# Output projections of a hybrid decoder block: residual with tokens on partitions, two projections by seven products, and weight parts made by accumulating DMAs

## The chip, the cores and the metric

The kernel runs on one core of a Trainium2 chip. The metric is the time of one execution on the device in microseconds; it is compared by the median of several runs. Engines are named as in the profile: PE is TensorE (matmuls; PEld its weight loads), DVE is VectorE, ACT ScalarE, POOL GpSimd, SP SyncE.

## What is computed

One decoder block on 512 tokens of width 1024, in float32, then a final norm:

```python
h = h + hybrid_mixer(rmsnorm(h), ...)            # 1024 -> ... -> [y_ssd | y_pool] (2048) @ w_out (2048 x 1024)
h = h + memory_cross_attention(rmsnorm(h), rmsnorm(mem), w_q, w_kv, w_o)   # 4 heads into 256 memory tokens
h = h + swiglu(rmsnorm(h), w_gate_up, w_down)    # width 2816
return rmsnorm(h, final_norm)
```

In the mixer, the first half of the concatenation, `y_ssd`, is a gated state-space result under an RMS norm of its own; the second, `y_pool`, comes from causal pooling. So the mixer's output is `rmsnorm(y) @ w_out[:1024] + y_pool @ w_out[1024:]`. Three matrices of 1024 x 1024 are the subject here: the pool half of `w_out` (stage **op**), its state-space half (**os**), and the attention's `w_o` (**wo**).

## The kernel before

**Precision.** Every float32 product is three TensorE matmuls of fp32r parts: high by high, high by low, low by high (`mm3`, L116). A weight block of 128 x 1024 (a *unit*) is loaded by SP into a `raw` buffer; ACT casts it to `whi` (L203) and DVE takes the difference as `wlo` (L205). There are 6 `raw`, 4 `whi` and 5 `wlo` buffers. Activations are split alike (`splits`: names end in h and l).

**Order.** `SPEC` is a table of slots; a slot is a line of items such as `os:3` or `k:0`. While the matmuls of a slot run, `advance` prepares the units of the next one, and the finishing steps (`post`) of the slot's items are woven between. Matmuls of one engine run in the order of the program.

**Strassen.** The FFN (stages g and d) and the attention's values (v) take seven products of half matrices in place of eight (`product`). Their weight blocks are four quarters of the matrix, numbered as forms 1 to 7; forms 3, 5, 6 and 7 are sums of quarters. The sums are made by an accumulating DMA that POOL issues (L172 loads a second quarter onto a `raw` buffer; L211 adds form 5 to form 1 and makes form 6 in a `wq` buffer) or by DVE (L190, L194: form 3). The activations' forms are made by `forms` (L1176). The products gather in the PSUM banks A (forms 1, 6, 7, 4), B (5, 3) and C (2), and DVE adds each bank to its two quarters of the result (`INTO`).

**The stages around the change** (with the time at which their matmuls begin in the profile):

- `op` (206.9): eight units, each 24 matmuls of 128 x 512. The result has features on partitions; `xT`, the input transposed, is added to it (L798).
- `os` (253.9): the same with `y`, which has been scaled and split before (`t_ygh`, `t_ygl`). The norm of `y` is a sum over partitions by two matmuls with ones (`ry`, L299) whose 128 x 512 result multiplies each unit's output (L329); L817 adds it to the residual. That is split for the attention (`t_hg`), and squares are added up for the next norm (`hacc`).
- `k` (297.7), `q` (321.0): keys and queries; the sums for the next norm (`r2`, two ones-matmuls) and four transposes (`r2t`) stand among them. Then the scores of four heads, their softmax, transposes of the probabilities (`pT`), and the products with the values (`o`, 12 matmuls for each half of a head).
- `wo` (410.0): eight units of 24; DVE adds each to the residual (L1048), ACT scales it for the FFN (L1054), and `forms` makes the FFN's forms. Between the last units the residual is turned by 32 transposes (`hT`, L1222) so that tokens are on partitions, as the FFN's drains want it, and its squares are summed by row.
- The FFN begins at 455.4 with product 1 of gate block 0 (`gA`).

Of the kernel before, what the change touches and what calls it, by code (L numbers as in the profile page):

```python
# [61 lines left out]
def hybrid_block(ctx: ExitStack, tc: tile.TileContext, a: dict, out: bass.AP,  # L62
# [119 lines left out]

    def split_unit(key):
        n = units[key][1]
        raw = ready[key]
# [21 lines left out]
        if key[0] == "s" and f == 2 and CHUNKS[c][:2] != ("g", 5):  # L207
            if (c, 5) not in sw:
                load_strassen(("s", c, 5))
            sw[c, 6] = sw.pop((c, 1))  # L210
            nc.gpsimd.dma_start(sw[c, 6][:, :n], sw[c, 5][:, :n], accum_op=ALU.add)  # L211
# [575 lines left out]
    def i_op(m):  # L787
        it = Item(keys=[("op", m)])

        def prep():  # L790
            it.x = T("x2")
            nc.sync.dma_start(it.x, a["xT"][m * P:(m + 1) * P, :])

        def mm():
            proj(hold(it, "op"), ready[("op", m)], [st["pg", k] for k in range(8)])

        def post():
            nc.vector.tensor_tensor(out=it.x, in0=it.x, in1=it.ps, op=ALU.add)  # L798
            st["hp", m] = it.x

        it.prep, it.mm, it.post = prep, mm, post
        return it

    rmsy = Rms("ry", "yacc")
    rms2 = Rms("r2", "hacc")
# [20 lines left out]


# [114 lines left out]
    def i_r2t():  # L942
        it = Item()

        def mm():
            pt = hold(it, "r2t")
            for c in range(NC):
# [611 lines left out]
```

## Time and profile before

| | us |
|---|---|
| median of 3 runs | 793.7 (793.55 to 793.85) |
| the profiled execution | 794.94 |
| its span on the core | 793.1 |
| mean granted TensorE clock in it | 0.997 |
| matmuls of `op` | 206.9 to 253.3 |
| matmuls of `os` | 253.9 to 297.5 |
| matmuls of `wo` | 410.0 to 454.8 |

A row of the groups reads: line, engine, operation, output and inputs by the program's names, shapes, count; then total busy time and mean duration in ns; then the idle time of the engine ahead of them and what ended it. A matmul's duration is longer than the step from one to the next, since they overlap. The time of a DMA is from its issue to its landing.

### The profile page before, as it was taken

How to read it: one execution, taken by the hardware profiler on the slowest of the kernel's cores; microseconds unless marked ns; L12 is line 12 of the kernel's file. 1: busy time of each engine (PE TensorE's matmuls, PEld its weight loads, DVE VectorE, ACT ScalarE, POOL GpSimd, SP SyncE). 2: the span in 40 equal slices, each digit the busy share in tenths (PEclk: the TensorE clock that was granted, in tenths of full speed). 3: DMA queues.
4: the chain of work that ended last, by engine and by line, in shares of the span. 5: the costliest groups of instructions: out<-in, count | busy, mean ns of one | idle time of the engine just before them, and what ended most of it. 6: DMA issues, size and time to landing. Idle time of an engine off the chain costs nothing.

```text
span 793.1 us, 10458 instructions
## 1 busy us (share of the span) xinstructions
PE 782.3 (99%) x3789; PEld 655.9 (83%) x3789; DVE 635.4 (80%) x944; ACT 499.6 (63%) x803; POOL 49.8 (6%) x66
## 2 busy tenths in 40 slices
PE   9999999999999999999999999999999999999996
PEld 7878888888888888888888888888888888888984
DVE  7999879999895798875766667788857798867897
ACT  8667699657953547555655695665445575455855
POOL 0000000000000000000000011011101011101000
PEclk9999999999999999999999999999999999999998
DMA  9235326134474234765455268787869798879702
GB/s 336 86 110 177 114 86 179 54 105 127 158 262 161 93 107 149 171 188 165 132 126 145 68 142 232 173 242 160 250 143 297 162 248 181 239 157 264 177 14 106
DMA packets 41283, 128.60 MB, mean 162 GB/s; under 512 B 4865, under 2 KB 7297, under 8 KB 41233
## 3 DMA queue, kind: packets, MB, share of 16 engines
q1 hardware_dynamic: 32880, 99.04, 36.9%
q0 software_dynamic: 8064, 28.58, 20.2%
q8 instruction: 29, 0.48, 0.2%
q10 hardware_dynamic: 288, 0.33, 0.1%
q14 instruction: 22, 0.17, 0.1%
HBM read 116.63 MB, written 2.13 MB: 150 GB/s over the span
## 4 chain that ended last, share of the span: by engine, by line
PE 84%; DVE 9%; DMA 3%; ACT 2%; issue 2%; SPq 0%; DVEq 0%
PE gA L1104 14%; PE gB L1104 8%; PE dA L1104 4%; PE gC L1104 3%; PE dB L1104 2%; DVE wlo L205 2%; PE vAB L1104 2%; PE k L889 2%; DVE t_hT L1263 2%; PE op L117 2%; PE wo L119 2%; PE op L118 2%; PE wo L117 2%; PE q L118 2%; PE q L117 2%; PE os L118 2%
## 5 line engine op out<-in xcount | busy, mean ns | idle before, releaser
L203 ACT CAST whi<-raw 128x1024 fp32r<-128x1024 f32 (+1 forms) x125 | 129.0, 1040 | 90.6 <-PE wo L118 11.8
L205 DVE TENSOR_TENSOR wlo<-raw,whi 128x1024 fp32r<-128x1024 f32 (+1 forms) x125 | 150.0, 1208 | 28.2 <-ACT whi L203 27.3
L203 ACT CAST whi<-wq 128x1024 fp32r<-128x1024 f32 (+1 forms) x76 | 77.4, 1028 | 74.5 <-PE dA L1104 17.8
L205 DVE TENSOR_TENSOR wlo<-wq,whi 128x1024 fp32r<-128x1024 f32 (+1 forms) x76 | 90.3, 1194 | 38.8 <-ACT whi L203 38.6
L172 POOL DMA_DIRECT2D raw<-w_s x38 | 32.7, 865 | 646.4 <-DMA raw<-w_s 521.6
L1104 PE MATMUL gA<-whi,t_xh 128*128 128x512 f32 (+1 forms) x192 | 71.7, 373 | 0.0
L1104 PE MATMUL gA<-wlo,t_xh 128*128 128x512 f32 (+1 forms) x192 | 71.4, 372 | 0.0
L1104 PE MATMUL gA<-whi,t_xl 128*128 128x512 f32 (+1 forms) x192 | 71.3, 371 | 0.0
L1104 PEld LDWEIGHTS gA<-whi,t_xh 128*128 128x128 f32 x192 | 36.2, 188 | 6.3
L1104 PEld LDWEIGHTS gA<-wlo,t_xh 128*128 128x128 f32 x192 | 36.2, 188 | 6.3
L1104 PEld LDWEIGHTS gA<-whi,t_xl 128*128 128x128 f32 x192 | 36.2, 188 | 6.1
L1120 ACT ACTIVATE t_gu<-t_gu,s 128x512 f32<-128x512 f32 (+1 forms) x24 | 16.4, 687 | 34.9 <-DVE t_gu L1116 34.9
L194 DVE TENSOR_TENSOR wq<-wq,wq 128x1024 f32<-128x1024 f32 (+1 forms) x19 | 22.5, 1194 | 16.7 <-DMA wq<-raw 16.7
L1104 PE MATMUL dA<-whi,t_xh 128*128 128x512 f32 (+1 forms) x91 | 34.7, 385 | 0.5 <-DVE t_hT L1263 0.3
L1104 PE MATMUL dA<-whi,t_xl 128*128 128x512 f32 (+1 forms) x91 | 34.8, 382 | 0.0
L1104 PE MATMUL dA<-wlo,t_xh 128*128 128x512 f32 (+1 forms) x91 | 34.6, 382 | 0.0
L1104 PE MATMUL gB<-whi,t_xq 128*128 128x512 f32 (+1 forms) x96 | 27.6, 371 | 0.0
L117 PE MATMUL z<-t_uh,whi 128*128 128x512 f32 x64 | 25.2, 394 | 0.6 <-ACT t_uh L233 0.6
L1182 ACT CAST t_xh<-t_x 128x512 fp32r<-128x512 f32 x30 | 18.6, 621 | 10.6 <-DVE t_x L1201 6.4
L117 PE MATMUL wo<-t_oh,whi 128*128 128x512 f32 x64 | 25.2, 394 | 0.0
L117 PE MATMUL v<-t_uh,whi 128*128 128x512 f32 x64 | 25.1, 392 | 0.0
L117 PE MATMUL q<-t_hgh,whi 128*128 128x512 f32 x64 | 25.1, 392 | 0.0
(406 smaller groups left out, 2224.6 us busy)
## 6 DMA issues: line engine op xcount, KB each, us to landing
raw<-w_u SPq DMA_DIRECT2D x68, 512.0 KB, 3.4
raw<-w_s SPq DMA_DIRECT2D x54, 512.0 KB, 4.5
wq<-w_s SPq DMA_DIRECT2D x36, 512.0 KB, 5.6
raw<-w_s POOLq DMA_DIRECT2D x36, 512.0 KB, 7.1
wq<-raw POOLq DMA_DIRECT2D x17, 512.0 KB, 8.2
t_x<-xT SPq DMA_DIRECT2D x16, 256.0 KB, 5.3
t_abc<-d_acs SPq DMA_DIRECT2D x16, 256.0 KB, 5.1
out<-t_hT SPq DMA_DIRECT2D x7, 256.0 KB, 2.1
```

Of the source, the lines that this page charges most:

```text
L117: nc.tensor.matmul(ps, whi, xhi, start=start, stop=False)
L118: nc.tensor.matmul(ps, whi, xlo, start=False, stop=False)
L119: nc.tensor.matmul(ps, wlo, xhi, start=False, stop=stop)
L172: nc.gpsimd.dma_start(sw[c, f][:, :n], quad("11" if f == 7 else "22"), accum_op=ALU.add)
L194: add = nc.vector.tensor_tensor(out=sw[c, 3][:, :n], in0=sw[c, 3][:, :n], in1=sw[c, 6][:, :n], op=ALU.add)
L203: nc.scalar.copy(hi[:, :n], raw[:, :n])
L205: nc.vector.tensor_tensor(out=lo[:, :n], in0=raw[:, :n], in1=hi.bitcast(F32)[:, :n], op=ALU.subtract)
L889: nc.tensor.matmul(it.ps[d], wh[:, ws], both, start=k == 0, stop=False, skip_group_check=True)
L1104: nc.tensor.matmul(it.ps[tt][:, o:e], p[:, ts_], w[:, ws], start=first, stop=(c, i, n) == pairs[-1] and p is xh and w is wl, skip_group_ch ...
L1120: st["silu"] = nc.scalar.activation(g, g, AF.Silu, scale=st["r3",][:, c:c + 1])
L1182: nc.scalar.copy(h if w is None else h[:, w], src)
L1263: d = nc.vector.tensor_tensor(out=h[:, half], in0=h[:, half], in1=it.ps[tt][:, half], op=ALU.add if sign > 0 else ALU.subtract)
```

## The change

The residual is kept with tokens on partitions from the start: eight tiles `h[c, r]` (128 tokens, half the features), loaded from `x` instead of `xT`.

- **op** stays plain but has tokens on its output's partitions: a unit covers two of eight feature blocks and one half of the output, and goes into four PSUM banks (`op`), which are drained into `h` after four units.
- **os becomes y, wo becomes o**, each by seven products (24 matmuls each, in the B and A and C banks; B is the double bank `pd`). The scaled `y` and the attention's outputs get their forms from a new function, `natural_forms`. The norm of `y` is four matmuls of one column and a short chain on 128 x 4 numbers (`rsqrt`); it is multiplied in by the drain. Form 1 and some others are cut into two items (`y:1.0`, `o:7.1`), one for each unit.
- **The features come back to partitions** for the attention by 32 new transposes (`hgT`), and for the FFN by the 32 of `hT`, now in the other direction. The sums of squares come from ACT on `h` (`sq`); the matmuls of `r2` and the transposes `r2t` are gone.
- **Low parts by DMA.** For 14 units (the last four of `op`, forms 7 and 4 of y and of o, form 5 of the first gate block) ACT casts the weight to `hi` as before, writes its negative, rounded alike, into `lo`, and POOL adds the raw weight to `lo` by an accumulating DMA. `early` starts them up to three units ahead.
- **Sums by DMA.** Form 3 of y, o and the first gate block is made by a third accumulating DMA (`wq<-wq`, L218) in place of the DVE addition.

```diff
+DMA_LOW = [('op', 4)]
+DMA_LOW_FORMS = {'y0': (4, 7), 'o0': (4, 7), 'g0': (5,)}
+DMA_SUM = ('y0', 'o0', 'g0')
...
-    "P:7", "op:0 g:5 op:1 op:2 g:6", "op:6 g:4 op:3 g:7", "op:5 op:4 ys", "op:7 yr", "os:0 ml", "os:1", "os:2",
-    "os:3 mm", "os:4", "os:5", "os:6", "os:7", "k:0", "k:1 r2", "k:2 vf:0", "k:3 rt vf:1", "q:0 vf:2 vf:3", "q:1 V:1", "q:2 V:2",
-    "q:3 S:0 V:5", "q:4 V:6",  "q:5 S:1 T:0 V:3", "q:6 S:2 T:1", "q:7 V:7 T:2", "V:4 S:3 O:0", "O:1", "T:3 O:2", "O:3", "o:0", "o:1",
...
+    "P:7", "op:0 g:5 op:1 op:2 g:6", "op:3 g:4 op:4 g:7 yf:0", "op:5 op:6 yf:1", "op:7 yf:2", "yr yf:3 ml", "y:1.0", "y:2.0", "y:5.0",
+    "y:1.1 y:2.1", "y:5.1 mm", "y:6", "y:3", "y:7 hg:0 hg:1", "y:4 hg:2 hg:3", "k:0", "k:1 hg:4 hg:5", "k:2 hg:6 hg:7 vf:0 sq:2.0",
+    "k:3 vf:1 sq:2.1", "q:0 vf:2 vf:3", "q:1 V:1", "q:2 V:2",
+    "q:3 S:0 V:5", "q:4 V:6",  "q:5 S:1 T:0 V:3", "q:6 S:2 T:1", "q:7 V:7 T:2", "V:4 S:3 O:0", "O:1", "o:1.0 T:3 O:2",
+    "o:5.0 O:3", "o:2.0", "o:1.1 o:2.1", "o:5.1", "o:6", "o:3", "o:7.0", "H:0 H:1 o:7.1", "H:2 H:3 o:4.0", "o:4.1",
...
+    def early(key):
...
+        hi = whi_p.tile([P, 1024], F32R, tag="hi", name=nm("whi"))
+        lo = wlo_p.tile([P, 1024], F32R, tag="lo", name=nm("wlo"))
+        nc.scalar.copy(hi[:, :n], raw[:, :n])
+        nc.scalar.activation(lo[:, :n], raw[:, :n], AF.Copy, scale=-1.0)
+        nc.gpsimd.dma_start(lo.bitcast(F32)[:, :n], raw[:, :n], accum_op=ALU.add)
...
+        if f in (2, 5) and CHUNKS[c][0] + str(CHUNKS[c][1]) in DMA_SUM and (c, 6) in sw and (f == 5 or (c, "5") in sw):
+            sw[c, 3] = sw.pop((c, 2))
+            nc.gpsimd.dma_start(sw[c, 3][:, :n], sw[c, 6][:, :n], accum_op=ALU.add)
...
-            t = mul("ot", it.ps, st["ry",])
-            h = st["hp", m]
-            nc.vector.tensor_tensor(out=h, in0=h, in1=t, op=ALU.add)
...
+                nc.vector.scalar_tensor_tensor(out=h, in0=it.ps[tt], scalar=st["ry",][sign][:, c:c + 1], in1=h,
+                                               op0=ALU.mult, op1=ALU.add)
...
+        H1 = cast(E, a_)
+        HO = cast(O)
+        M = T("x57")
+        nc.vector.tensor_tensor(out=M[:, a_], in0=E[:, a_], in1=E[:, b_], op=ALU.subtract)
+        nc.vector.tensor_tensor(out=M[:, b_], in0=O[:, b_], in1=E[:, b_], op=ALU.subtract)
+        yield
+        rest(H1[:, b_], E[:, a_], H1[:, a_])
+        LO = T("xl", F32R)
+        rest(LO, O, HO)
...
+        H2 = cast(M)
+        N = T("x64")
+        nc.vector.scalar_tensor_tensor(out=N[:, a_], in0=M[:, a_], scalar=-1.0, in1=O[:, b_],
...
+        nc.vector.scalar_tensor_tensor(out=N[:, b_], in0=N[:, a_], scalar=-1.0, in1=O[:, a_],
...
+        H3 = cast(N)
+        L2 = T("xl", F32R)
+        rest(L2, M, H2)
...
+        L3 = T("xl", F32R)
+        rest(L3, N, H3)
...
+            for key in plan[spos:spos + 3]:
+                early(key)
```

What this moves, at three places. In the program's order PE has 3756 matmuls instead of 3776, DVE 991 instructions instead of 946, ACT 814 instead of 774.

**PE, the end of os.** Before, the last unit of `os` is followed at once by the first key matmuls:

```order
L117 MATMUL os_2935<-t_ygh_2290,whi_2877 128x512
L118 MATMUL os_2935<-t_ygl_2293,whi_2877 128x512
L119 MATMUL os_2935<-t_ygh_2290,wlo_2878 128x512
L889 MATMUL k_2987<-t_mn_2769,whi_2918 128x512
L890 MATMUL k_2987<-t_mn_2769,wlo_2919 128x256
```

Now, at the change from product 7 of y to product 4 (`whi_605`, `wlo_606` and `whi_608`, `wlo_609` are the two units of form 4; both low parts come by DMA):

```order
L1213 MATMUL yA_563_2668<-wlo_595_2819,t_xh_534_2560 128x512
L948 MATMUL hgT_612_2945<-ident_88,t_h_451_2177 128x128
L948 MATMUL hgT_612_2945<-ident_88,t_h_452_2179 128x128
L948 MATMUL hgT_612_2945<-ident_88,t_h_453_2182 128x128
L948 MATMUL hgT_612_2945<-ident_88,t_h_454_2184 128x128
L948 MATMUL hgT_613_2950<-ident_88,t_h_451_2177 128x128
L948 MATMUL hgT_613_2950<-ident_88,t_h_452_2179 128x128
L948 MATMUL hgT_613_2950<-ident_88,t_h_453_2182 128x128
L948 MATMUL hgT_613_2950<-ident_88,t_h_454_2184 128x128
L1213 MATMUL yA_562_2667<-whi_605_2878,t_xh_490_2295 128x512
L1213 MATMUL yA_562_2667<-whi_605_2878,t_xl_496_2310 128x512
L1213 MATMUL yA_562_2667<-wlo_606_2879,t_xh_490_2295 128x512
```

The transposes of the residual's first half stand inside the y stage, and `wlo_609` is read nine matmuls into product 4.

**PE, the head of wo.** Before, the last head's attention product is wholly ahead of `wo`, which starts from the first head's parts:

```order
L119 MATMUL o_4070<-t_Ph_4043,t_Vl_3975 128x512
L117 MATMUL o_4070<-t_Ph_4045,t_Vh_3893 128x512
L118 MATMUL o_4070<-t_Pl_4056,t_Vh_3893 128x512
L119 MATMUL o_4070<-t_Ph_4045,t_Vl_3901 128x512
L117 MATMUL wo_4089<-t_oh_3971,whi_4051 128x512
L118 MATMUL wo_4089<-t_ol_3989,whi_4051 128x512
```

Now the first o product begins after head 1's attention product (`o_887`), ahead of the last head's probability transposes (`pT`), and the two are woven (`t_xh`, `t_xl` are forms of the attention's output):

```order
L125 MATMUL o_887_4116<-t_Ph_828_3895,t_Vl_746_3510 128x512
L123 MATMUL o_887_4116<-t_Ph_829_3897,t_Vh_797_3777 128x512
L124 MATMUL o_887_4116<-t_Pl_840_3920,t_Vh_797_3777 128x512
L125 MATMUL o_887_4116<-t_Ph_829_3897,t_Vl_808_3800 128x512
L1213 MATMUL oA_901_4152<-whi_868_4066,t_xh_876_4083 128x512
L1213 MATMUL oA_902_4153<-whi_868_4066,t_xh_876_4083 128x512
L1123 MATMUL pT_903_4166<-ident_88,t_p_865_4059 128x128 x2
L1123 MATMUL pT_903_4166<-ident_88,t_p_875_4080 128x128 x2
```

Four more matmuls of `oA`, four transposes `pT_904` and the first three of `oB` follow, then head 2's attention product. Two heads' attention products (24 matmuls) have moved behind the first matmuls of the projection.

**POOL, from wo into the FFN.** Before, its queue held second loads onto `raw` and two sums for the first gate block:

```order
L172 DMA raw_926_4307<-w_s 128x1024
L172 DMA raw_952_4419<-w_s 128x1024
L172 DMA raw_992_4574<-w_s 128x1024
L172 DMA raw_997_4596<-w_s 128x1024
L211 DMA wq_904_4206<-raw_926_4307 128x1024
L172 DMA raw_1024_4743<-w_s 128x1024
L211 DMA wq_935_4353<-raw_952_4419 128x1024
```

Now, from o's form 7 (`wlo_956`, `wlo_961`) over form 4 (`wlo_966`, `wlo_969`) to form 5 of the first gate block (`wlo_990`, `wlo_1026`):

```order
L205 DMA wlo_956_4371<-raw_937_4279 128x1024
L205 DMA wlo_961_4383<-raw_945_4307 128x1024
L205 DMA wlo_966_4420<-raw_948_4341 128x1024
L178 DMA raw_1040_4721<-w_s 128x1024
L178 DMA raw_1046_4748<-w_s 128x1024
L205 DMA wlo_969_4453<-raw_951_4349 128x1024
L205 DMA wlo_990_4551<-raw_964_4416 128x1024
L215 DMA wq_954_4368<-raw_964_4416 128x1024
L218 DMA wq_959_4380<-wq_954_4368 128x1024
L205 DMA wlo_1026_4678<-raw_975_4499 128x1024
```

`wlo_969` stands behind two second loads, the later of which goes into a buffer that `wlo_961` reads; `wlo_1026` stands behind two sums, and the second sum waits for the first. POOL's queue has 32 more DMAs in all.

More of the change, by code (lines that the diff above doesn't have):

```diff
@@ L206, in split_unit @@
         ready[key] = (hi, lo)
[L207 to L211, printed above, removed]
+        if key[0] == "s":
+            sums(key)
         yield
@@ L794, in mm @@
         def mm():
[L795 to L805 removed]
+            if k == 0:
+                st["op"] = [PS("op") for _ in range(NC)]
+            it.ps = st["op"]
+            wh, wl = ready[("op", j)]
@@ new lines, in mm @@
+            for c in range(NC):
+                cs = slice(c * P, (c + 1) * P)
+                for n in range(2):
+                    ws = slice(512 * n, 512 * n + 512)
+                    xh, xl = st["pg", 2 * k + n]
+                    mm3(it.ps[c], xh[:, cs], xl[:, cs], wh[:, ws], wl[:, ws], k == 0 and n == 0, k == 3 and n == 1)
+        def post():
+            for c in range(NC):
+                h = st["h", c, r]
+                nc.vector.tensor_tensor(out=h, in0=h, in1=it.ps[c], op=ALU.add)
+                yield
@@ new lines, in post, with i_y @@
+            st["ry",] = {1: p, -1: n}
+        it.mm, it.post = mm, post
+        return it
+    def i_y(f, part=None):
+        it, ends, _ = product("y", 0, f, part)
+        def post():
+            yield from need("ry")
+            r, k, sign = INTO[f]
+            for tt in range(2):
+                c = 2 * k + tt
+                h = st["h", c, r]
+                nc.vector.scalar_tensor_tensor(out=h, in0=it.ps[tt], scalar=st["ry",][sign][:, c:c + 1], in1=h,
+                                               op0=ALU.mult, op1=ALU.add)
+                yield
+        it.post = post if ends else None
+        return it
@@ L824, in i_os, with i_hg, mm, post @@
+    def i_hg(m):
+        it = Item()
+        def mm():
+            pt = hold(it, "hgT")
+            for c in range(NC):
+                nc.tensor.transpose(pt[:, c * P:(c + 1) * P], st["h", c, m // 4][:, (m % 4) * P:(m % 4 + 1) * P], ident)
+        def post():
+            yield from splits([("hg", m)], [("hg", 512)], [it.ps], col(V_XAT + m))
         it.mm, it.post = mm, post
@@ L940, in i_q @@
         return it
[L942 to L947, printed above, removed]
-                nc.tensor.transpose(pt[:, c * P:(c + 1) * P], st["r2",][:, c * P:(c + 1) * P], ident)
-        def post():
-            s = SM("r2s", [P, NC])
-            nc.vector.tensor_scalar(out=s, in0=it.ps.rearrange("p (c l) -> p c l", l=P)[:, :, 0],
-                                    scalar1=1.0 / 16.0, scalar2=None, op0=ALU.mult)
-            st["r2s",] = s
-        it.mm, it.post = mm, post
-        return it
     def i_score(h):
@@ L1497, in _pack @@
     wo = g["w_out_mix"]
-    u += [mtile(wo[1024:], m) for m in range(8)]
-    u += [mtile(wo[:1024], m) for m in range(8)]
+    wp = wo[1024:].reshape(4, 2, P, 2, 512)
+    u += [wp[k, :, :, r].transpose(1, 0, 2).reshape(P, 1024) for r in range(2) for k in range(4)]
     wkv = g["w_kv"]
@@ L1502, in _pack @@
     u += [mtile(g["w_q"], m) for m in range(8)]
-    u += [mtile(g["w_o"], m) for m in range(8)]
     w_u = np.stack([f(t) for t in u])
```

201 lines of the change are left out of this document (135 added, 66 removed), and 3 rows, old and new, of the table SPEC.

## The prediction

> **What bounds the kernel now.** I read the page's busy times first, then TensorE's waits, then a table of stretches.
>
> ```profile
> PE 782.3 (99%) x3789; PEld 655.9 (83%) x3789; DVE 635.4 (80%) x944; ACT 499.6 (63%) x803; POOL 49.8 (6%) x66
> ...
> PE 84%; DVE 9%; DMA 3%; ACT 2%; issue 2%; SPq 0%; DVEq 0%
> ...
> PE warm L384 <- DVE ones L100: 1.2, 1, 1.2
> PE z L117 <- ACT t_uh L233: 0.6, 1, 0.6
> PE yo L119 <- DVE t_prl L241: 0.4, 1, 0.4
> PE dA L1104 <- DVE t_hT L1263: 0.3, 1, 0.3
> PE gB L1104 <- DVE wlo L205: 0.2, 1, 0.2
> ```
>
> TensorE is busy in 99% of the span and 84% of the chain that ended last is its own. All its waits on other engines come to 2.7 us (the five rows added). So a matmul taken away comes off the time, as long as the engines that feed it still keep up; and there is nearly no wait left to remove. How near the feeders are to their limit stands in the stretches (columns: PE, PEld, DVE, ACT, POOL busy, then clock, DMA share, GB/s):
>
> ```profile
> 170.00:206.90 36.90, 36.49 (x190) 30.98 (x189) 34.71 (x59) 28.43 (x59) 0.00 (x0) 1.00 0.42 131
> 206.90:253.90 47.00, 47.00 (x220) 39.36 (x220) 35.11 (x51) 27.52 (x46) 0.00 (x0) 1.00 0.60 212
> 253.90:297.70 43.80, 43.80 (x195) 36.28 (x195) 36.05 (x58) 22.77 (x36) 0.00 (x0) 1.00 0.30 97
> 388.70:410.00 21.30, 21.24 (x113) 18.07 (x112) 17.70 (x30) 15.48 (x28) 1.70 (x2) 1.00 0.65 173
> 410.00:455.40 45.40, 45.40 (x210) 37.54 (x209) 26.08 (x42) 23.69 (x44) 2.55 (x3) 1.00 0.37 93
> ```
>
> The second row is `op`, the third `os`, the last `wo`. In all three TensorE never stops and its granted clock is 1.00. VectorE has 12 us to spare beside `op`, 8 beside `os`, 19 beside `wo`; 2.2 in the stretch ahead of `op`.
>
> **What the change takes from TensorE.**
>
> ```profile
> L117 PE MATMUL os<-t_ygh,whi 128*128 128x512 f32 x64 | 24.9, 389 | 0.0
> L117 PE MATMUL wo<-t_oh,whi 128*128 128x512 f32 x64 | 25.2, 394 | 0.0
> ...
> 474.05 5.44 PE gA L1104 x24
> ...
> L299 PE MATMUL ry<-t_ryh,ones_r x1: 389/389/389, 253.5 to 253.5; 128*128 128x512 f32 x1
> L948 PE MATMUL r2t<-ident,t_r2t x4: 270/272/273, 320.6 to 320.9; 128*128 128x128 f32 x4
> 458.38 0.87 PE hT L1222 x8
> ```
>
> `os` and `wo` are three lines of 64 matmuls each, 192 apiece. Seven of eight products are left, 168 apiece, of the same size: 48 fewer. A matmul lasts 389 ns, but they overlap: 24 back to back take 5.44 us in the chain, so 0.2267 us is what one costs. That is 48 x 0.2267 = **10.9 us**. The norms' sums go too: two 512-wide matmuls for `ry`, two alike for `r2`, 4 x 0.2267 = 0.9; and four transposes `r2t`. Eight transposes take 0.87, so 0.109 each: 0.4. Added are 32 transposes `hgT` (3.5 us) and four matmuls of one column for `ry`. The profile has no such matmul; it costs between nothing and a 512-wide one, so 0 to 0.9 for the four; I take the rate of a transpose, which also loads 128 columns, 0.4. The turn `hT` keeps its 32. `op` changes its layout but keeps 8 x 24 matmuls. Sum: 10.9 + 0.9 + 0.4 - 3.5 - 0.4 = **8.3 us** less TensorE work.
>
> **What the feeders must do now.** The rows that price it:
>
> ```profile
> L205 DVE TENSOR_TENSOR wlo<-raw,whi 128x1024 fp32r<-128x1024 f32 x122 | 148.0, 1221 | 28.2 <-ACT whi L203 27.3
> L1186 DVE TENSOR_TENSOR t_xl<-t_x,t_xh 128x512 fp32r<-128x512 f32 x30 | 19.9, 686 | 0.3
> L243 DVE SCALAR_TENSOR_TENSOR t_ygl<-t_y,vec,t_ygh 128x512 fp32r<-128x512 f32 x8 | 6.0, 747 | 0.1
> L241 DVE TENSOR_TENSOR t_ol<-o,t_oh 128x512 fp32r<-128x512 f32 x8 | 5.4, 689 | 2.5 <-ACT t_oh L233 2.4
> L1191 DVE TENSOR_TENSOR t_x<-t_fa,t_fb 128x256 f32<-128x256 f32 x15 | 6.3, 421 | 1.2 <-ACT t_fa L1169 0.9
> L203 ACT CAST whi<-raw 128x1024 fp32r<-128x1024 f32 x122 | 127.5, 1050 | 90.6 <-PE wo L118 11.8 <-PE gA L1104 10.8 <-PE op L118 10.5
> ```
>
> *Beside `op`*: a set of natural forms is five 256-wide and three 512-wide VectorE operations, 5 x 0.421 + 3 x 0.686 = 4.2 us; `yf` brings four sets, 16.6 us. Four low parts leave for the DMA (4 x 1.22 = 4.9). 35.1 + 16.6 - 4.9 = 46.8 of 47.0 us. That is full by mean durations; back to back a 512-wide operation costs some 0.60 (below, 1.29 for two), about a tenth less, and work may reach ahead into the y stage. The eight `ygl` (6.0 us) fall away too, but most of them stand ahead of this stretch, so I credit none. I count no wait here and keep it as a rival. *Beside y*: 14 low parts instead of 8, four of them by DMA, so 2.4 us more, while 14 drains at about 0.7 take the place of 16 operations on `os`; it stays inside the 8 us spare, which is the cover; without it, it would cost its own 2.4. ScalarE gains 14 casts against 8 and four copies for the DMA, 10 x 1.05, beside 21 us spare. *Beside o*: 16.6 for its forms instead of 5.5 for the eight `t_ol` at 0.69, six more drains (4.1), 2.4 of low parts: 17.6 more against 19 spare, and part of it stands already in the stretch ahead. These cost nothing.
>
> *The third y product.* The order shows that its second pair's high part can be cast only when the product before it has ended, and is needed six matmuls (1.4 us) later, the low part ten later (2.3): cast 1.05, then 1.22 for the low part, 2.27. Bounds 0 and 0.3 (a handover's latency); I take **0.2**.
>
> *The head of o.* Before, `wo` began only after head 3's attention product, 24 matmuls later than now. Now the first o product stands in front of that head's probability transposes and takes its forms from heads 0 and 1.
>
> ```profile
> 397.61 1.49 DVE L983 TENSOR_REDUCE mx<-sc 128x2 f32<-128x512 f32 x2
> ...
> 401.83 1.29 DVE L241 TENSOR_TENSOR t_ol<-o,t_oh 128x512 fp32r<-128x512 f32 x2
> 403.22 0.62 DVE L997 TENSOR_SCALAR t_p<-t_p,rs 128x256 f32<-128x256 f32 x2
> ```
>
> From the last score (about 398.3, where the second maximum begins) to the finished probabilities (403.84) it took 5.5 us. TensorE has 24 matmuls, 5.4 us, in that gap, then two of o (5.9), then wants probabilities, then low parts of o's forms. Two 256-wide operations stand on VectorE ahead of the last probabilities (6.3 after the score; TensorE is there at 6.2), one before the first low part (6.75 against 6.3), four more before the second form (8.95 against 8.3): together 1.1 us by durations, 0.5 at the faster pace. Ends: 0, and 2.4 if one weight low part (1.22) gets ahead. I take **0.9**.
>
> *Low parts by DMA.* Fourteen leave VectorE: an ACT copy, then an accumulating transfer that GpSimd issues. How long such a transfer takes here:
>
> ```profile
> raw<-w_s POOLq DMA_DIRECT2D x36, 512.0 KB, 7.1
> wq<-raw POOLq DMA_DIRECT2D x17, 512.0 KB, 8.2
> ...
> raw<-w_s POOLq DMA_DIRECT2D x4, 512.0 KB, 5.3
> wq<-raw POOLq DMA_DIRECT2D x2, 512.0 KB, 5.3
> ...
> DMA to landing us min/median/max: 3.3/7.8/11.7
> raw<-w_s SPq DMA_DIRECT2D x54, 512.0 KB, 4.5
> L211 POOL DMA_DIRECT2D wq<-raw x18: 846/852/864, 323.9 to 758.4; - x18
> ```
>
> Call it L: 7.1 and 8.2 are the kernel's medians, 5.3 (twice) those of 405 to 480 us, 3.3 and 11.7 the ends of the weight sums. Three places decide:
> - Product y:4's last low part. Its buffer is free six matmuls before y:3 ends; it is needed 36 matmuls and eight transposes later, 9.0 us. Copy 1.05, a handover 0.1, then L: late by L - 7.85.
> - o:4's. GpSimd's queue holds an accumulation into another raw buffer ahead of it; that one needs a load (4.5), which needs the buffer that o:7's low part frees. Copy 1.05 + L + 4.5 + 0.85 to issue + L, against 86 matmuls and 16 transposes, 21.2: late by 2L - 14.8.
> - The FFN's first form 5: two transfers in a row and two issues, 2L + 1.7, against 19.4: late by 2L - 17.7.
>
> At 5.3 and at 7.1 none is late, at 8.2 the three sum to 0.35 + 1.6 = 2.0, at 11.7 to 18. The new kernel moves more in these stretches than the old one did at 5.3; between 7.1 and 8.2 I take **0.6**.
>
> The Trainium skill speaks to this: "DMA: Bandwidth & Descriptors", in the section on the anatomy of a DMA on the SWDGE (gpsimd) path, fits 2.0 us plus the bytes over 436e3; by that page 512 KB is an estimated 3.2 us, the low parts never late, and the sum 0.6 better. The rows above disagree: only the least of 18 comes near, so the measured L stands.
>
> **Sum.** The profiled execution took 794.94 us, 1.24 over the median of 793.7 (its span is 793.1, the rest lies around it). 794.94 - 8.3 + 0.2 + 0.9 + 0.6 = 788.3 profiled, **787.1 us** as a median.
>
> **The rivals.**
> - *Everything is covered*, with no new wait: 793.7 - 8.3 = 785.4. For it, five waits in 793 us before; against it, the head of o, which has no slack by the rows.
> - *VectorE late at the first y products*, or the head of o at its upper end. For it the 46.8 of 47.0; against it, 8 us spare behind. One set of forms late is 4.2: 785.4 + 1.7 + 3 to 4.2, about 790.5.
> - *Slower: the accumulating transfers become the bound.* At L = 10 the three places are late by 2.15 + 5.2 + 2.3 = 9.7 us. With 1.1 from the others 785.4 + 10.8 = 796.2; it decides from L = 9.5, where the gain is gone. For it: 11.7 has occurred, and 32 transfers more go through one GpSimd queue, where each waits for the one ahead. Against it: 5.3 in this very stretch. The Trainium skill bears on its price: "TensorE: Matmul & The Clock Gate", on HAM oscillation, warns of TensorE gaps over about 3.4 us, after which the clock starts again at half. By an estimate from that page each such gap would cost some 1.7 us on top, so about 798 here. The quoted stretches show 1.00 and no such gap, so nothing here can confirm it.
> - *The change doesn't remove what it says*: the counts in the order show 48 fewer wide matmuls, so I give it nothing.
>
> **How the numbers follow.** Forecast with waits of 0.6 to 3 us (786.0 to 788.4): 0.52. All covered: 0.13. Late VectorE (788.4 to 792): 0.15. Gain eaten, 792.1 to 795.3: 0.07. Slower: 0.13. A measurement of this kernel tells some 0.2% (1.6 us) from no change; so faster 0.80, same 0.07, slower 0.13. The range goes from 785.0 (a little under all covered) to 793.0, which leaves out the slower case and most of the eaten gain.
>
> **What would show it.** TensorE's busy time down by 8.3 us; its waits on other engines at about 4.4 instead of 2.7 us, the largest on forms of o (`t_xh`, `t_xl`) and on `wlo`; the accumulating `wlo<-raw` at 5 to 8 us to landing. A wait of several us at `yA`, `oA` or `gB` for a DMA of `wlo` would mean the slower rival; waits at `yA` for `t_xh` or `t_xl`, the late VectorE. The forecast is wrong if a matmul of y or o starts further apart than 0.2267 us, or if new waits pass 4 us.

## The result, and the profile after

| | us |
|---|---|
| before, median of 6 runs beside it | 793.79 (793.55 to 794.74) |
| after, median of 6 runs | 811.55 (810.28 to 813.16) |
| ratio | 1.0221, interval 1.0208 to 1.0235 |
| profiled execution of after, its span | 811.5, 809.8 |

The change makes the kernel 17.8 us slower; 6.6 us faster had been forecast. The page of the kernel after, busy times and the chain that ended last:

```profile
PE 784.5 (97%) x3773; PEld 652.9 (81%) x3773; DVE 643.0 (79%) x989; ACT 528.5 (65%) x851; POOL 77.3 (10%) x98
...
PE 67%; DVE 12%; DMA 10%; ACT 6%; issue 3%; POOL 0%; DVEq 0%; POOLq 0%; ACTq 0%; SPq 0%
```

TensorE has fewer matmuls and is yet busy longer, which shows that the sum of durations isn't the work: a matmul at a lower clock lasts longer (0.63 us below, against 0.39 in the prediction's rows). So I measured the work by the steps: from each start to the next, less one step of that size (0.2267 us for 512 columns, 0.120 for 256, 0.109 for a transpose). What is left over is time lost, 15.6 us before and 40.4 after. Span less loss is 777.5 before and 769.4 after, 8.1 us less, and 24.8 us of loss came.

Two small things stand in the wrong sum there. The norm of `y` is not four matmuls of one column, as the description of the change and the prediction have it, but eight in the profile (`ry`, from 252.52). They start 0.112 us apart, and these 0.9 us are counted as loss. The stretch behind the last matmul's start, 0.7 us longer after, is counted as work. By the count of matmuls in the two traces it is 52 fewer of 512 columns (11.8 us), 28 more transposes (3.1) and the eight of `ry` (0.9): **7.8 us of work did go**. TensorE's own share of the chain fell from 84 to 67%, and the DMA's rose from 3 to 10%.

TensorE's largest waits after (total, times, longest):

```profile
PE oA L1213 <- DMA wlo<-raw: 5.1, 1, 5.1
PE rm L341 <- ACT t_rmh L326: 3.7, 1, 3.7
PE yA L1213 <- DMA wlo<-raw: 2.1, 1, 2.1
PE yC L1213 <- DVE t_h L862: 1.6, 1, 1.6
```

All waits come to 15.9 us, against 2.7. Two of the four largest are for low parts by DMA, at the places where the prediction had put its queue (y:4, o:4). The second, `rm`, is the sum of squares of the memory tokens, of which the prediction says nothing. The same stretches as before (PE, PEld, DVE, ACT, POOL busy, clock, DMA share, GB/s):

```profile
206.90:253.90 47.00, 46.92 (x223) 38.96 (x222) 34.39 (x61) 31.51 (x54) 6.85 (x8) 1.00 0.90 254
253.90:300.00 46.10, 38.33 (x162) 30.01 (x160) 35.26 (x62) 29.60 (x44) 5.96 (x7) 0.96 0.77 197
300.00:325.00 25.00, 25.00 (x139) 21.64 (x140) 18.30 (x32) 17.96 (x37) 1.61 (x2) 0.93 0.63 199
420.00:460.00 40.00, 38.21 (x175) 30.81 (x173) 29.21 (x47) 28.62 (x41) 8.61 (x10) 1.00 0.79 198
460.00:490.00 30.00, 26.51 (x114) 21.54 (x115) 18.57 (x33) 19.99 (x40) 5.15 (x6) 0.89 0.91 201
```

Beside `op` the DMA engines went from 0.60 to 0.90 of their time; VectorE is far from full there (34.4 of 47). The granted clock, 1.00 in all these stretches before, fell to 0.96, 0.93 and 0.89. The DMA issues on POOL's queue (KB each, median us to landing):

```profile
raw<-w_s POOLq DMA_DIRECT2D x44, 512.0 KB, 7.8
wq<-raw POOLq DMA_DIRECT2D x21, 512.0 KB, 9.8
wlo<-raw POOLq DMA_DIRECT2D x14, 512.0 KB, 8.4
```

**The wait of oA**, from the timelines of POOL, SP and PE (start, duration; in brackets the idle time before and its releaser):

```profile
439.01 0.86 POOL L205 DMA_DIRECT2D wlo<-raw  x1 [1.77 <-DVE t_h L1163]
...
453.65 0.85 POOL L178 DMA_DIRECT2D raw<-w_s  x1 [3.01 <-DVE t_h L1163]
454.18 2.08 POOL L205 DMA_DIRECT2D wlo<-raw  x2
```

```profile
447.77 0.33 SPq L167 DMA_DIRECT2D raw<-w_s  x1
```

```profile
463.33 0.80 PE L1213 MATMUL oA<-wlo,t_xh 128*128 128x512 f32 x1 [5.12 <-DMA wlo<-raw]
463.92 0.63 PE L1213 MATMUL oA<-whi,t_xh 128*128 128x512 f32 x1
464.35 0.63 PE L1213 MATMUL oA<-whi,t_xl 128*128 128x512 f32 x1
...
468.38 0.40 PE L1213 MATMUL gA<-wlo,t_xh 128*128 128x512 f32 x1
```

It is the chain that the prediction's queue describes. A low part is issued at 439.01 and lands after 8.71, at 447.72; at 447.77 SP can load into the buffer that this freed; the load lands after 5.30 (453.07); POOL, which had been held by it, issues its second load at 453.65 and o:4's low part at 454.18; that lands after 9.10, and TensorE goes on at 463.33.

The last lines show a second price. After the gap the matmuls start 0.43 us apart instead of 0.2267, for nine steps: 1.8 us more.

**The wait of rm.** SP's timeline, then ScalarE's:

```profile
240.21 1.51 SPq L961 DMA_DIRECT2D t_mem<-memT  x3
256.83 0.33 SPq L186 DMA_DIRECT2D raw<-w_u  x1
257.21 1.89 SPq L961 DMA_DIRECT2D t_mem<-memT  x4
266.89 0.33 SPq L186 DMA_DIRECT2D raw<-w_u  x1
267.27 0.42 SPq L961 DMA_DIRECT2D t_mem<-memT  x1
```

```profile
251.26 0.42 ACT L362 ACTIVATE t_macc<-t_mem 128x256 f32<-128x256 f32 x1 [8.37 <-DMA t_mem<-memT]
```

SP's waits from 240 to 258, and two pieces of the chain that ended last:

```profile
SPq L186 <- DMA wq<-raw: 11.6, 1, 11.6
SPq L186 <- DVE t_macc L366: 3.7, 1, 3.7
```

```profile
240.76 12.88 DMA t_mem<-memT
...
257.21 4.03 DMA t_mem<-memT
```

Three of the eight memory tiles are asked for at 240 and take 11 to 13 us to land. Behind them in SP's order stands a plain weight load. It waits 11.6 us for an accumulating transfer that still reads its `raw` buffer, then 3.7 for VectorE, which is itself held at the sum of the first tiles' squares. Four of the other tiles stand behind that load until 257, and the last one behind a second such load until 267. ScalarE takes its work in order too: it sat 8.37 us on the first tile, with the casts of y's forms behind it. The rows of the squares' high part say when its cast, of 0.4 us, begins, before (first fence) and after:

```profile
L284 ACT CAST t_rmh<-t_macc x1: 405/405/405, 256.1 to 256.1; 128x256 fp32r<-128x256 f32 x1
```

```profile
L326 ACT CAST t_rmh<-t_macc x1: 399/399/399, 275.6 to 275.6; 128x256 fp32r<-128x256 f32 x1
```

In both kernels TensorE wants them at 272 to 276. Before they were there 19 us early; all of that cover was used up. The first tile is also asked for later now: before, SP issued the eight from 229.6 to 250.8, one or two behind each weight load.

### The profile page after: what moved, and what is told of

It reads as the page before. It is cut to its first block, busy times and chain, and to the rows that moved or that the text cites. A ratio compares the mean times of both kernels' runs of the same rounds, so it can differ in the third digit from the quotient of the medians.

```text
span 809.8 us, 10631 instructions
## 1 busy us (share of the span) xinstructions
PE 784.5 (97%) x3773; PEld 652.9 (81%) x3773; DVE 643.0 (79%) x989; ACT 528.5 (65%) x851; POOL 77.3 (10%) x98
## 3 DMA queue, kind: packets, MB, share of 16 engines
HBM read 122.92 MB, written 2.13 MB: 154 GB/s over the span
## 4 chain that ended last, share of the span: by engine, by line
PE 67%; DVE 12%; DMA 10%; ACT 6%; issue 3%; POOL 0%; DVEq 0%; POOLq 0%; ACTq 0%; SPq 0%
PE gA L1213 12%; PE gB L1213 6%; PE dA L1213 4%; DVE wlo L250 3%; DMA t_mem<-memT 3%; DMA raw<-w_s 3%; DMA wq<-raw 3%; PE gC L1213 2%; PE dB L1213 2%; PE xbc L125 2%; PE xbc L124 2%; PE xbc L123 2%; DMA wlo<-raw 2%; PE vAB L1213 2%; PE k L1017 2%
## 5 line engine op out<-in xcount | busy, mean ns | idle before, releaser
L250 DVE TENSOR_TENSOR wlo<-raw,whi 128x1024 fp32r<-128x1024 f32 (+1 forms) x107 | 127.9, 1205 | 33.3 <-ACT whi L248 32.5
L248 ACT CAST whi<-raw 128x1024 fp32r<-128x1024 f32 (+1 forms) x107 | 109.8, 1038 | 64.5 <-issue 11.1
L250 DVE TENSOR_TENSOR wlo<-wq,whi 128x1024 fp32r<-128x1024 f32 (+1 forms) x92 | 109.8, 1197 | 42.2 <-ACT whi L248 41.9
L248 ACT CAST whi<-wq 128x1024 fp32r<-128x1024 f32 (+1 forms) x92 | 94.2, 1031 | 74.6 <-PE dA L1213 17.8
L1213 PE MATMUL gA<-whi,t_xl 128*128 128x512 f32 (+1 forms) x144 | 53.5, 372 | 0.0
L1229 ACT ACTIVATE t_gu<-t_gu,r 128x512 f32<-128x512 f32 (+1 forms) x24 | 16.3, 687 | 35.3 <-DVE t_gu L1225 35.3
L1213 PE MATMUL gB<-whi,t_xh 128*128 128x512 f32 (+1 forms) x96 | 36.3, 378 | 0.8 <-ACT whi L248 0.6
L1213 PE MATMUL gB<-wlo,t_xh 128*128 128x512 f32 (+1 forms) x96 | 35.9, 377 | 0.1
L1213 PE MATMUL gB<-whi,t_xl 128*128 128x512 f32 (+1 forms) x96 | 35.7, 372 | 0.0
L215 POOL DMA_DIRECT2D wq<-raw x22 | 20.1, 911 | 66.2 <-DVE wlo L250 57.4
```

The lines of the kernel that those rows point to most:

```text
L248: nc.scalar.copy(hi[:, :n], raw[:, :n])
L250: nc.vector.tensor_tensor(out=lo[:, :n], in0=raw[:, :n], in1=hi.bitcast(F32)[:, :n], op=ALU.subtract)
L1213: nc.tensor.matmul(it.ps[tt][:, o:e], p[:, ts_], w[:, ws], start=first, stop=(c, i, n) == pairs[-1] and p is xh and w is wl, skip_group_ch ...
L1229: st["silu"] = nc.scalar.activation(g, g, AF.Silu, scale=st["r3",][:, c:c + 1])
```

## The experiments

Sixteen kernels ran. All were compared with the kernel before on the same chip, which stood at 793.8 to 794.2 throughout; the kernel after is at 811.55.

### The low parts: all, op's alone, the forms' alone

```diff
-DMA_LOW = [('op', 4)]
-DMA_LOW_FORMS = {'y0': (4, 7), 'o0': (4, 7), 'g0': (5,)}
+DMA_LOW = []             # e1, e3
+DMA_LOW_FORMS = {}       # e1, e4
```

> All 14 low parts are made by VectorE again; the weight sums stay on DMAs. Theory (late accumulating DMAs): the waits of oA (5.1 us) and yA (2.1 us) for wlo go, and with them the slow matmuls behind each (granted clock 0.63 to 0.69 in those stretches, about 1.7 us each), so 811.5 falls by 11 to 12 us to about 800. If the memory loads were late because of the transfers' traffic, the 3.7 us wait of rm goes too, with its slow matmuls and the waits at the first y products, some 9 us more: about 791. Rival (VectorE cannot carry them, 14 x 1.22 = 17 us more): new waits for wlo by VectorE at op and y, and the time stays above 806.

> Only the four low parts of op go back to VectorE; those of y, o and the gate block stay on DMAs. If the traffic beside op (DMA share 0.90) is what makes the memory tiles late: rm's wait shrinks and the time falls by 5 to 9 us, to 803 to 806. If it is the order of SyncE's queue: about 811, or a little more for VectorE's 4.9 us. The waits for wlo at y:4 and o:4 stay.

> Only the ten low parts of y, o and the first gate block go back to VectorE; the four of op stay on DMAs. Theory: the waits for wlo at y:4 and o:4 and the slow matmuls behind them go (11 to 12 us), rm's wait stays: about 800. Rival (VectorE): new waits in the y stage, 805 or more.

e1: 798.59, ratio 1.0052 (1.0037 to 1.0067). e3: 811.08, 1.0206 (1.0184 to 1.0227). e4: 800.96, 1.0086 (1.0069 to 1.0103). So the 14 low parts by DMA cost **13.0 us**, the ten of the forms nearly all of it (10.6). e1 and e4 are where their theories put them (about 800). With the low parts on VectorE (e1) the waits for `wlo` by DMA are gone, and this is left at the top:

```profile
PE rm L341 <- ACT t_rmh L326: 4.0, 1, 4.0
PE gB L1213 <- ACT t_fT L1374: 1.3, 1, 1.3
```

The wait of `rm` is no child of the low parts, so e1's further hope of 791 is refuted. Of e3's two outcomes, 803 to 806 for the traffic beside op and 811 for the order in SP's queue, it is the second. e3 says that op's four cost nothing, yet in it the wait of `yC` went and that of `oA` grew to 7.4 us: what is gained ahead of o:4 is waited off there. By stages the loss (start-to-start excess, as above) is:

```
us from      206.9   262   285   300   395   420   460   500   sum of the whole kernel
before         0.1   0.0   0.0   0.2   0.1   0.2   0.3   0.2   15.6
after          3.8   5.9   2.6   1.8   1.2   5.9   4.8   1.7   40.4
e4             3.7   5.5   0.3   0.1   1.2   0.4   2.7   2.0   29.0
e3             1.6   6.1   0.6   0.0   1.2   8.1   6.0   2.9   40.0
e1             1.5   6.6   0.1   0.0   1.3   0.4   2.7   2.4   27.6
```

206.9 is op and the head of y (with the 0.9 us of `ry`'s matmuls in every row but the first), 262 holds `rm`, 285 and 300 y:4, 395 the head of o, 420 o:4, 460 and 500 (to 550) the head of the FFN; the slow steps behind o:4 fall into 460. The column of 262 doesn't move in any of the three.

### The memory tiles: earlier, or wanted later

```diff
-    "P:7", ... "yr yf:3 ml", ...
+    "P:7 ml", ... "yr yf:3", ...                # e2
-    "y:1.1 y:2.1", "y:5.1 mm", "y:6",
+    "y:1.1 y:2.1", "y:5.1", "y:6 mm",           # e5, e7 (e7 with e1's edit)
```

> Only the item that loads the attention's memory and squares it is moved from the slot ahead of y to the slot ahead of op. Theory (the memory tiles arrive late, ScalarE waits for them in order, and the y forms, the residual's additions and rm wait behind): the rm wait (3.7 us), its slow matmuls (1.7) and the waits at the first yA and yC (2 to 3 us) go: about 803. The waits for wlo at y:4 and o:4 stay at 2 and 5 us. Rival (VectorE is late by its own load beside op): yA and yC wait as before and only rm changes: about 806.

> The changed kernel with one edit: the item with the two matmuls of rm stands one slot later, beside y's product 6 instead of its form 5. Theory (the memory tiles land when they land; rm only asked for them 4 us too early): rm's wait of 3.7 us and the slow matmuls behind it (1.7 us) go, 811.5 becomes about 806; yC's wait of 1.6 us, y:4's 2.1 and o:4's 5.1 stay. Rival (ScalarE and VectorE are late as a whole there): the wait moves to y:6 or y:3 and the time stays above 809.

> All low parts by VectorE (as in e1, 798.6) and rm one slot later. Theory: rm's 4.0 us and its slow matmuls (1.8 us) go from 798.6: about 793, the same as before or just faster. Rival: VectorE, busy 42 of 47 us beside op, is what is late, and the wait only moves: 797.

e2: 822.56, 1.0351 (1.0336 to 1.0367), a miss: the tiles' loads and squares now stand ahead of stage P's own work on their engines. Its waits open with a new one:

```profile
PE pd L123 <- DVE t_y L731: 13.0, 1, 13.0
```

e5: 806.36, 1.0161 (1.0136 to 1.0185), as its theory said; rm's wait is gone. e7: 798.24, 1.0049 (1.003 to 1.0068), a miss (793 was expected) and no better than e1, although rm's wait is gone there too:

```profile
PE hgT L948 <- DVE t_h L917: 1.7, 2, 1.4
PE yA L1213 <- DVE t_h L917: 1.4, 1, 1.4
...
PE yB L1213 <- DVE t_h L917: 0.8, 1, 0.8
```

Asking for `rm` later moves the late work behind it into y's last products, and VectorE's drains come late in its place. From this I read for a while that VectorE has no room beside y. e14 below shows that this was wrong.

### o:4's low part ahead of the gate's transfers in POOL's queue

```diff
-            nc.gpsimd.dma_start(sw[c, f][:, :n], quad("11" if f == 7 else "22"), accum_op=ALU.add)
+            d = nc.gpsimd.dma_start(sw[c, f][:, :n], quad("11" if f == 7 else "22"), accum_op=ALU.add)
+            if f == 7 and CHUNKS[c][:2] == ("g", 0):
+                after(d, st["lo dma", ("s", CHUNKS.index(("o", 0, (2, 3), 512)), 4)])
...
-        nc.gpsimd.dma_start(lo.bitcast(F32)[:, :n], raw[:, :n], accum_op=ALU.add)
+        st["lo dma", key] = nc.gpsimd.dma_start(lo.bitcast(F32)[:, :n], raw[:, :n], accum_op=ALU.add)
```

> The changed kernel with one edit: in GpSimd's queue the last low part of o's form 4 stands ahead of the two second loads for the gate's form 7 instead of behind them; the same transfers are made. Theory (the head of the queue): it is issued some 6 us sooner, lands before 458, and oA's wait of 5.1 us and the slow matmuls behind it (2.3 us) go: about 804. Rival (the DMA engines are full there, share 0.9 to 1): it lands later than 8.4 us after its issue and 2 us or more of the wait stay: 807 or more.

812.84, 1.0238 (1.0216 to 1.026), a miss. The wait of `oA` is gone, and nothing is gained:

```profile
PE gA L1215 <- ACT t_gu L1237: 3.0, 1, 3.0
PE gB L1215 <- DMA wlo<-raw: 2.3, 1, 2.3
```

The transfers set back by this are the gate's own, and TensorE waits for them 15 us later: for the low part of its form 5, and for `t_gu`, which ScalarE makes only after 9.0 us of idle time ahead of a cast whose weight sum (`wq<-raw`) lands at 483.5. The DMA engines were at 0.79 and 0.91 of their time in these stretches in the kernel after, and this order only chose another consumer to be late.

### The head of the FFN, and low parts by DMA one stage at a time

```diff
-    "U:0.5.0", "U:0.1.1", "U:0.2.1", "U:0.5.1 sq:3.0", "U:0.6 sq:3.1",
+    "U:0.5.0", "U:0.1.1 sq:3.0", "U:0.2.1 sq:3.1", "U:0.5.1", "U:0.6",     # e8, on e7
+DMA_LOW_FORMS = {'y0': (4, 7)}                 # e9, on e8
+DMA_LOW_FORMS = {'y0': (4, 7), 'g0': (5,)}     # e10, on e8
+DMA_LOW = [('op', 4)]                          # e12, on e8
```

> As e7, and the squares for the FFN's norm three slots earlier (beside product 1 of the first gate block instead of 5 and 6). Theory: the waits of gA for t_gu (0.9 us) and gB for wlo (0.6 us) at 510 to 534 come from ScalarE and VectorE being late with them: 1 to 1.5 us less than e7, about 791.5. Rival: ScalarE gets the squares where it makes the FFN's forms, and gB's wait for t_fT grows by as much: the same as e7 or slower.

> As e8, but the four low parts of y's forms 7 and 4 are made by accumulating DMAs again; those of op, o and the gate block stay with VectorE. Theory (beside y it is VectorE that is late once it makes all low parts itself: 5.9 us of waits there in e7, against 0.4 for y:4's transfer in e5): VectorE loses 4.9 us of work there, the waits of hgT, yA and yB for the residual (4 us) go, and y:4 waits under 0.5: e8's 796.7 becomes about 792.5, faster than before. Rival (these waits come from the memory's normalization, which stands at the same place): only 1 us less, about 796.

> As e9, and the two low parts of the first gate block's form 5 by DMA too. Theory: VectorE is late beside the FFN's forms by these two (2.4 us), so the waits of gB for t_fT (1.3) and gA for t_gu (1.2) shrink, while with o's transfers gone the low parts land in time: 1.5 us less than e9, about 791. Rival (accumulating transfers are late there whatever else runs): gB waits for wlo by DMA, 2 us or more with slow matmuls behind it, 795.

> Against e8 (796.7) the last four low parts of op go by DMA again, nothing else. Theory (VectorE is late beside y because it carries too much beside op): 4.9 us less for VectorE there clear the waits of hgT, yA and yB for t_h (4.0 us together with a little of slow clock), and the time falls to 791 to 794, no slower than before. Rival (beside y each of VectorE, ScalarE and the DMA engines is without slack, so a wait only changes its name): the waits at t_h become waits for whi, wlo or t_mem, and the time stays at 796 to 799.

e8: 796.68, 1.0031 (1.0019 to 1.0042). e9: 798.90, 1.0061 (1.0048 to 1.0074). e10: 800.88, 1.0091 (1.0074 to 1.0108). e12: 798.71, 1.0058 (1.0044 to 1.0073). Moving `sq:3` gained 1.6, roughly: e7's runs lie between 796.3 and 800.1. Each group of low parts that went back to the DMA cost some 2 us by itself: y's 2.2, the gate's 2.0 more (roughly again, e10's runs lie between 798.9 and 804.0), op's 2.0; for the theory that VectorE is the limit all three are misses. In e10 the wait that came is `gA`'s for `t_gu`, 4.1 us, and the chain in front of it is a weight sum by DMA, as in e6 (`wq<-raw`, 10.1 us). e9's waits show the trade: those for `t_h` went, and these came:

```profile
PE yA L1213 <- DMA wlo<-raw: 1.9, 1, 1.9
PE yB L1213 <- ACT whi L248: 1.6, 2, 1.3
```

### The memory tiles on another queue

SP's order can be taken out without touching when `rm` is wanted: the eight loads are issued by ScalarE's DMA queue, all ahead of the squares. This changes two things at once, the queue and the time at which the tiles are asked for.

```diff
-                nc.sync.dma_start(mt, a["memT"][k * P:(k + 1) * P, :])
-                sq_acc("macc", mt, n=MEM)
+                nc.scalar.dma_start(mt, a["memT"][k * P:(k + 1) * P, :])
                 st["mem"].append(mt)
+            for mt in st["mem"]:
+                sq_acc("macc", mt, n=MEM)
                 yield
```

> Against the changed kernel only the memory tiles' loads move: all eight are issued by ACT's queue, ahead of their squares, instead of one by one by SP's. Theory (order on SP's queue: a weight load that waits for a raw buffer stands ahead of five of the eight): all eight are issued at about 243 us and have landed by about 257; the wait of rm for t_rmh falls from 3.7 us to under 1, the slow matmuls behind it go, and the time falls by 3 to 6 us, to 805 to 808. Rival (the transfers beside op are limited by what the DMA engines move, whoever issues them): they land 11 to 14 us after issue or later, rm still waits 2 us or more, and the time stays at 810 to 813. A third outcome would be that rm's wait goes and the time does not, since the next feeder (VectorE at t_h) takes the wait over.

> e1's edit (all low parts on VectorE) and e11's (the memory tiles' loads issued by ACT's queue). Theory queue order: e1's wait of rm for t_rmh (4.0 us, with slow matmuls some 6 us) goes and nothing takes its place; 798.6 - 5 to 6.6 = 792 to 793.6. Rival (no slack on VectorE beside y): rm's wait goes, waits of yA, yB or hgT for t_h of 3 to 5 us come, as in e7; 796 to 798.5.

> e13 and the two sums of squares sq:3 moved two and three slots earlier at the head of the FFN, which took 1.6 us off between e7 and e8. Theory: 1 to 2 us below e13, in the best case 790.5 to 792, faster than before. Rival: another wait at gA or gB takes its place, within 0.5 us of e13.

e11 (on the kernel after): 806.18, 1.0152 (1.0135 to 1.0169). e13 (with e1's edit): 792.55, 0.9989 (0.998 to 0.9997). e14 (with e8's move of `sq:3` as well): **791.87, 0.9973 (0.9964 to 0.9982)**, 1.9 us under the kernel before. e11 and e13 are where their theories put them. e14 is 0.7 under e13, between its theory (1 to 2) and its rival (0.5), and not resolved: a wait of `gB` for `wlo` (1.5) went and one of `gA` for `t_gu` (1.2) came. e13's tiles are asked for within 3.5 us, and the cast of the squares begins at 258.6 instead of e1's 273.7:

```profile
L961 ACTq DMA_DIRECT2D t_mem<-memT x8: 335/447/574, 243.2 to 246.7; - x8
...
L326 ACT CAST t_rmh<-t_macc x1: 399/399/399, 258.6 to 258.6; 128x256 fp32r<-128x256 f32 x1
```

That is 5.4 us on the kernel after and **6.0 us** on e1: moving eight small loads was worth three quarters of what the change took from TensorE. Was it the other queue or the earlier asking? In e11 the tiles are asked for from 238.3 to 249.6 and take longer to land than in the kernel after (4.0/5.5/12.9), yet the wait of `rm` is gone:

```profile
DMA to landing us min/median/max: 6.1/12.5/14.6
```

So there it was the time of asking, and no faster landing. Where y's stage was thought full, e14 shows room (its page, waits and stretch):

```profile
PE 776.1 (98%) x3773; PEld 650.3 (82%) x3773; DVE 658.5 (83%) x1003; ACT 514.7 (65%) x836; POOL 65.2 (8%) x84
```

```profile
PE gB L1214 <- ACT t_fT L1375: 1.3, 1, 1.3
PE gA L1214 <- ACT t_gu L1236: 1.2, 1, 1.2
```

```profile
253.90:300.00 46.10, 46.10 (x220) 38.51 (x221) 42.61 (x67) 26.25 (x38) 1.70 (x2) 1.00 0.61 181
```

Beside y VectorE does 42.6 us in 46.1, with all low parts, and TensorE never stops. So VectorE's lateness in e7 and e8 was not a lack of room; most likely it was the late memory tiles handed on. That is not isolated: e14 differs from e8 in the queue of the tiles and also in the slot of `rm`.

### On that base: y's low parts by DMA, and form 3 by VectorE

```diff
+DMA_LOW_FORMS = {'y0': (4, 7)}     # e16, on e14
-DMA_SUM = ('y0', 'o0', 'g0')
+DMA_SUM = ()                       # e17, on e14
```

> e14 with the low parts of y's forms 4 and 7 by DMA again. Theory that VectorE limits y and the low parts by DMA relieve it: waits at t_h go, 1 to 2 us below e14. Rival (the accumulating transfers come late there): a wait of yA for wlo of 1 to 2.5 us and of yB for whi, 2 to 3 us above e14, as between e8 and e9 (2.2).

> e14 with form 3 of y, o and the first gate block summed by VectorE, as before the change, instead of by a third accumulating transfer: 6 transfers fewer, 6 additions of 128x1024 (about 1.3 us each) more on VectorE. Theory that VectorE is the limit beside y: 1 to 3 us above e14, waits at t_h or wlo. Rival that the transfers are the limit: 1 to 2 us below e14. If the time is the same, neither is.

e16: 796.01, 1.0024 (1.0012 to 1.0035): 4.1 us over e14, so even where the queue order is mended the low parts of y alone lose, as the rival said and by more than its 2 to 3. Its profiled execution is one of the two quickest of eleven (793.42; clock 0.997) and has

```profile
PE yA L1214 <- DMA wlo<-raw: 1.8, 1, 1.8
```

with no slow matmul behind it; the other nine took 795.7 to 797.7 at clocks of 0.993 to 0.996. That a slightly longer gap costs them the clock is likely, but they have no profile.

e17: 798.87, 1.0068 (1.0054 to 1.0082): 7.0 us over e14, where 1 to 3 were expected. On this base the third accumulating transfers **gain** 7 us. With the sums on VectorE it is late not beside y, as the theory had it, but at the end of o:

```profile
PE hT L1371 <- DVE t_h L1164: 3.8, 1, 3.8
```

## Why the prediction was wrong

**TensorE's work: right.** 8.3 us forecast, 7.8 by count and 8.1 by the steps (e14 the same: 790.5 of span less 21.4 of loss is 769.1). The difference of 0.5 is `ry`: eight matmuls of 0.112 where the sum had four of 0.109.

**The low parts by DMA: the step that failed.** The sum has 0.6 us for them; they cost 13.0 (e1). The queues were drawn rightly, and named the two places that waited; the sizes put into them were wrong in three ways.
- *L.* Taken at 7.1 to 8.2 from the kernel before; here `wlo<-raw` landed in 8.4 us (median; 4.5 to 11.2), and at o:4 in 8.71 and 9.10. The prediction said that the new kernel moves more in these stretches, and kept the old number. By its own formula for o:4 (copy 1.05 + L + 4.5 + 0.85 + L against 21.2), the measured 8.71 and 9.10, the load's 5.30 and 1.16 for the handover and the issues give 4.1 us late against 0.5 at the middle of its L; 5.1 was measured, and the last 1.0 I did not follow. At y:4 L - 7.85 gives 0.9 with the 8.75 that was measured; the wait was 2.1.
- *The clock.* A gap was priced at its length. Behind the gaps of y:4 and o:4 came 7 and 9 slow steps of 0.2 us extra, 3.2 us, and behind that of `rm` 7 more, 1.4. The text knew this only in the rival's estimate, and that was about the right size: 1.7 us for each gap.
- *The neighbours.* Only the consumers of the low parts were asked whether they would be late. With them SP's first memory tiles took 11 to 13 us to land (3.6 to 3.7 in e1), ScalarE stood behind them, and y's head was late: 3.8 us of loss in the first column, 1.5 without low parts. By the stages the loss that e1 takes away (12.8) is thus o:4 with 7.6 (columns 420 and 460), y:4 with 4.3 (285 and 300) and y's head with 2.3, less some 1.4 elsewhere.

**The memory tiles: not in the prediction at all.** 6.0 us (e13 against e1), a term put at nothing without a reason. The prediction placed the new work beside y and o and asked each engine for its spare time; it did not ask what stands in SP's order ahead of the memory loads, though the change asks for them 10 us later and moves accumulating transfers, which hold `raw` buffers, into that place. It drew POOL's queue and not SP's.

**VectorE beside op and y: right in its result, not in its sum.** "Full by mean durations" (46.8 of 47.0), yet it was busy for 34.4 in the kernel after, and its work cost next to nothing in e14: 1.5 us more loss beside op than before, 0.9 of it `ry`'s matmuls, and none beside y. The forms took 16.4 us in e14 (16.6 worked out), but the stretch had 41.7 with all low parts on VectorE: four `ygl` (3.0 us) stood in it after all, for which the text gave no credit, and some work of its neighbours fell outside. e7 seemed to contradict this step; e14 shows that the room is there.

**The head of o: right.** 0.9 forecast; 1.2 of loss from 395 to 420, against 0.1 before, 0.4 of it at a product of the values just ahead. What is left, 0.8, comes as forecast from late forms of o: TensorE's weight loads wait 0.4 for `t_xl` and 0.2 for `t_xh`. **The third y product**: 0.2 forecast; in e14 no column of y from 262 on loses more than 0.2.

**Form 3 by DMA**: held to cost nothing, which is right, but for a reason the text did not give: on VectorE it would have cost 7.0 us (e17). Not all accumulating transfers are alike. Form 3 has whole products of time to land: y's two sums land at 258.7 and 272.6 in the kernel after, and its product begins at 283.8. A low part is wanted within one: y:4's last lands at 299.86, two microseconds after TensorE wanted it.

**The head of the FFN: missed.** The drains and copies there (`t_fT` by ScalarE, `t_gu` by ScalarE or VectorE) make gaps of 0.9 to 1.3 us in e1, e7, e8, e13 and e14, all without low parts by DMA. They were not in the sum.

**The rivals.** The slower one named the right mechanism and place, and gave 796.2 from L = 10, with 0.13 of the chance. Its threshold (9.5) was reckoned without the clock and without the memory tiles; L of 8.4 to 9.1 was enough. The prediction's own tell-tale held: it named waits at `yA` and `oA` for `wlo` as the sign of this rival, and new waits over 4 us as the sign that the forecast is wrong.

What it comes to: 793.8 - 7.8 of work + 13.0 low parts + 6.0 memory tiles + 0.7 for `sq:3` (e13 to e14, not resolved well) + 5.9 of what is left (786.0 to 791.9) gives 811.6. The sum must close, since each term is the step from one run to the next; it says what each edit was worth in this order. The 5.9 is mostly the head of the FFN (`gB`'s wait for `t_fT` begins at 459, so it stands in column 420) and the head of o, as the stages of e14 show:

```
us from      206.9   262   285   300   395   420   460   500   sum of the whole kernel
e13            1.6   0.2   0.1   0.1   1.1   1.7   1.2   3.4   23.7
e14            1.6   0.2   0.1   0.1   1.1   1.7   1.7   1.4   21.4
```

**Still open**: on e1's base, whether the 6.0 us come from the earlier asking alone, as e11's 5.4 do, or partly from faster landing; that e13's tiles land in 2.4 to 5.4 us and e1's in 3.6 to 8.0 hints at some of the latter. Whether a slot for the loads between e2's, which is far too early, and the changed kernel's would have done as well on SP's queue was not tried. And why o:4 and y:4 waited 1 us longer than their chains.

## What to carry to other kernels

Work that is moved from an engine to a transfer isn't free because the engine was the fuller one: ask by when it must land, price the landing at the traffic that will be there and not at today's, and follow every queue that its buffer holds up, the plain loads' queue too. A load that waits for a buffer holds all loads behind it in its queue; small loads that are wanted at a fixed time belong on another queue or a little ahead of it (far ahead, in e2, cost 11 us). When removing a wait leaves the time the same, look for one late source that hands its delay on before concluding that every engine is full.
